# A decoder layer on one core: FFN products that add up in shared PSUM banks, and modulation sums moved ahead

## The chip, the cores and the metric

The kernel runs on one core of a Trainium2 chip. The metric is the device time of one execution in microseconds (us). The engines are TensorE (PE, matmuls; PEld is its weight load), VectorE (DVE), ScalarE (ACT), GpSimd (POOL) and SyncE (SP, whose queue issues the DMAs). PSUM has eight banks of 128 x 512 f32, into which PE writes.

## The reference, cut to what matters

One layer of a decoder: 1024 tokens, width 1024, f32. A conditioning vector `c` gives six modulation rows (`mod = silu(c) @ w_ada + b_ada`): shift, scale and gate for the mixer and for the FFN.

```
mod = c_act @ w_ada[l] + b_ada[l]
sh_m, sc_m, gt_m, sh_f, sc_f, gt_f = ...split(mod, 6)
h = rms_norm(x, g_pre_mix) * (1 + sc_m) + sh_m
x = x + gt_m * rms_norm(mixer(h), g_post_mix)
h = rms_norm(x, g_pre_ffn) * (1 + sc_f) + sh_f
up = h @ w_up                      # 1024 x 5632: gate | val
gate = conv3(gate) + conv_b        # causal, depthwise, along the tokens
y = (gelu_tanh(gate) * val) @ w_down
x = x + gt_f * rms_norm(y, g_post_ffn)
```

The mixer is one input projection, twelve heads of dilated window attention in three groups, a pooling group and an output projection.

## The kernel before, in words

Every f32 matmul operand is split into a high part of type fp32r (`copy`, on ACT) and the low rest (`lower`, `split`, on DVE), and each product is three matmuls: high x high, high x low, low x high (L1044 to L1046 in the FFN's first half, L1344 to L1346 in its second).

**Start** (to 62 us): adaLN columns, first norm, transposes, first projection.

**Attention phase** (to about 385 us): six units, each a pair of heads. `project(un, prev)` runs 8 x 8 groups of three matmuls (L222 to L224); after each group the queue `Q` ticks one slot and runs the tasks that are due: scores (L655), softmax, transposes (L675), weighted sums (L685), merges. PE's program is in the order written; the other engines' order in this phase is set by a scheduler by priority, and earlier code has the higher priority. In units 2, 3 and 4 (`MU = 2`) three modulation rows are computed as well, in halves `hf` of 512 columns: mixer gate (`mod_row`), FFN shift and FFN scale (`mod_col`). `mod_acc` loads eight 128 x 512 blocks into two buffers `mraw` (L485), multiplies and adds them on DVE into one buffer `macc` (L487, L489). PE then sums over partitions with a matmul of ones, 20 slots (first half) and 48 slots (second half) into the unit: L504 for the row, after a split of `macc` into `mah` and `mal`, L519 for columns. The row goes on with two broadcast loads and L508.

**Middle** (385 to 447 us): output projection, norms, transposes of h into the 2 x 2 blocks of the FFN's operand, and the first products.

**FFN, first half** (447 to 860 us): 22 units `c` of 2 x 128 columns (gate and value). Each is a 2 x 2 block product in Winograd's form with seven products instead of eight: `(n, c)`, n = 1 to 7, of 12 matmuls each. Products 1 and 2 run one to three units ahead. `steps` is PE's order: `(5,c) (4,c-1) (6,c) (2,k) (1,k) (3,c) (7,c)`, and for the first and last units `(5,c) (6,c) (4,c-1) (3,c) (7,c)`; the last step is `(4,21)`, right behind `(7,21)`. Each product has a bank of its own, from the list `idle`. `evac(n, c)` adds it on DVE into tiles in SBUF one step later (L1053 to L1063), with `UU` for the sum that several results share; `first(c)` copies product 1 on ACT and adds product 2. After product 4 comes the gate's chain: `cv` on ACT (L1064), two taps on DVE (L1154, L1156), GELU on ACT (L1158), times the value on DVE (L1161, `gated`). `act_sum` (L1173) forms the sums of two units that the second half needs, and SP stores them in `gscr`. All four engines follow the order written here. At the last five steps `prep_down` starts to load and split operands of the second half.

The FFN's gate row is computed in this half too (`gate_acc`, L1197, one block at a step; `gate_sum`, L1204), from unit 14 on.

**FFN, second half** (860 us to the end): again seven products, order `DOWN = (1, 2, 6, 5, 3, 7, 4)`, each over 11 blocks k and 4 blocks of tokens t, in two groups of four banks by turns. `out_sum` adds them up, `y_half` and `y_end` make the last norm, the gate and the residual (L1350 to L1366). In the last product the blocks of tokens end one after another.

Of the kernel before, what the change touches and what calls it, by code (L numbers as in the profile page):

```python
# [79 lines left out]
MU = 2  # L80
# [7 lines left out]
GATE_AT = 16  # L88
# [11 lines left out]
def block_kernel(ctx: ExitStack, tc: tile.TileContext, x, pos, cols, rows, consts, w_ada_a, w_ada_b, w_in_u,  # L100
# [411 lines left out]

    def mod_col(s, mb, hf, use, later):
        acc = mod_acc(s, hf)
        m = bank(mb)

        def fin():
            for i in range(4):
                nc.tensor.matmul(m[:, i:i + 1], acc[:, i * P:(i + 1) * P], ones[:, 0:1], start=True, stop=True)  # L519
            use(m[:, 0:4], slice(4 * hf, 4 * hf + 4))  # L520

        later(fin)
# [51 lines left out]
    with tc.tile_pool(name="bp", bufs=1) as bp, tc.manual_schedule(engines={ET.PE}):  # L574
# [210 lines left out]

        prev = None
        for ui in range(5):
# [11 lines left out]
            if MU <= ui <= MU + 2:  # L799
                for hf in range(2):  # L800
                    due = Q.slot + MLAG[hf]
                    later = lambda f, ahead=False, due=due: Q.at(due - MSPL * ahead, f)
                    if ui > MU:
                        mod_col(ui - MU, 7, hf, fin_shift if ui == MU + 1 else fin_scale, later)
                    elif hf:
                        Q.after(MLAG[0] + 1, lambda later=later: mod_row(0, 2, 6, gtg, 7, 1, later))
                    else:
                        mod_row(0, 2, 6, gtg, 7, 0, later)
# [7 lines left out]
        wps.append(load_piece(w_in_p[0], 1024))  # L816
        attend(un, Q.slot + 24)
# [27 lines left out]
    if True:  # L845
# [88 lines left out]
        with tc.manual_schedule(engines={ET.PE, ET.Activation, ET.DVE, ET.Pool}):  # L934
# [61 lines left out]
            UU = cp.tile([P, 2, 512], F32, name="UU", tag="gtg")  # L996
# [10 lines left out]

            def start_piece(n, src):
                W[n, 0] = new_piece()
                split(src, *W[n, 0])  # L1010
# [25 lines left out]
            def product(n, c):  # L1036
                a, w = USES[n]
                wh, wl = W.pop((w, c))
                used[n, c] = idle.pop(0)
                o = bank(used[n, c])  # L1040
                for k in range(4):
                    ks = slice(k * P, (k + 1) * P)
                    ah, al = side(a, k)
                    nc.tensor.matmul(o, wh[:, ks], ah, start=k == 0, stop=False)  # L1044
                    nc.tensor.matmul(o, wh[:, ks], al, start=False, stop=False)  # L1045
                    nc.tensor.matmul(o, wl[:, ks], ah, start=False, stop=k == 3)  # L1046
# [3 lines left out]
            def evac(n, c):  # L1050
                u, v = UU[:, c % 2], VV[c % 3]
                if n == 6:
                    nc.vector.tensor_sub(u, u, done_with(6, c))  # L1053
                    nc.vector.tensor_add(v[:, hi], u, done_with(5, c))
                elif n == 3:
                    nc.vector.tensor_add(v[:, lo], v[:, hi], done_with(3, c))
                elif n == 7:
                    o = done_with(7, c)
                    nc.vector.tensor_add(u, u, o)
                    nc.vector.tensor_add(v[:, hi], v[:, hi], o)  # L1060
                elif n == 4:
                    g = GG[:, c % 2]
                    nc.vector.tensor_add(g[:, hi], u, done_with(4, c))  # L1063
# [17 lines left out]
            first(1)  # L1081
# [3 lines left out]
            product(3, 0)  # L1085
            sums(hi_t, (3,))
# [8 lines left out]
            evac(6, 0)  # L1095
            start_sum("t4", b21, b21, t2r)
            evac(3, 0)
# [6 lines left out]
    gtf_d = tc.dram_tile([1, D], F32, name="gtf_d")  # L1104
    with tc.manual_schedule(engines={ET.PE, ET.Activation, ET.DVE, ET.Pool}):
# [4 lines left out]
        def fetch(src, low=True):  # L1110
# [3 lines left out]
            if low:  # L1114
                lower(r, *w)
            return w if low else (w, r)

        def lower(r, wh, wl):
            nc.vector.tensor_tensor(wl, r, wh.bitcast(F32), ALU.subtract)  # L1119
# [5 lines left out]
        def prep(n, c):  # L1125
# [10 lines left out]
            elif n in (1, 2):  # L1136
                w, r = fetch(w_up[c, :, n - 1], False)
                W[n, c] = w
                return lambda: lower(r, *w)
# [10 lines left out]
            copy(nc.scalar, w[0], src)  # L1150
            return lambda: lower(src, *w)
# [17 lines left out]
        def act_sum(c, i):  # L1169
            g0, g1 = VV[(c - 1) % 3], VV[c % 3]  # L1170
# [6 lines left out]
        for c in range(NC_FF):  # L1177
# [7 lines left out]
            if c in SKIP or not ahead:  # L1185
                steps += [(5, c), (6, c)] + old + [(3, c), (7, c)]
            else:
                steps += [(5, c)] + old + [(6, c)] + ahead + [(3, c), (7, c)]
        steps.append((4, NC_FF - 1))

        def gate_acc(hf, kb):
            raw, acc = gm[:, 0], gm[:, 1]
            nc.sync.dma_start(raw, w_ada_b[3, hf, kb])
            if kb == 0:
                nc.vector.tensor_scalar_mul(acc, raw, cact2[:, 0:1])
            else:
                nc.vector.scalar_tensor_tensor(acc, raw, cact2[:, kb:kb + 1], acc, op0=ALU.mult, op1=ALU.add)  # L1197
            if kb == 7:
                nc.sync.dma_start(raw[0:1], rows[5:6, hf * 512:(hf + 1) * 512])

        def gate_sum(hf, c):
            used["gate", c] = idle.pop(0)
            o = bank(used["gate", c])
            nc.tensor.matmul(o, ones, gm[:, 1], start=True, stop=True)  # L1204
            row, g, sl = gm[0:1, 0], gm[0:1, 1], slice(hf * 512, (hf + 1) * 512)
            nc.sync.dma_start(g, rows[7:8, sl])

            def add():
                nc.vector.tensor_tensor(row, done_with("gate", c)[0:1], row, ALU.add)

            def fin():
                nc.vector.scalar_tensor_tensor(row, row, -1.0 if hf else 1.0, g, op0=ALU.mult, op1=ALU.mult)
                nc.sync.dma_start(gtf_d[:, sl], row)

            at_step(now[0] + 1, add)
            at_step(now[0] + 3, fin)
# [12 lines left out]
        def finish_4(c):  # L1229
            i, g, v = now[0], GG[:, c % 2], VV[c % 3]  # L1230
# [9 lines left out]
        for hf, c in ((0, GATE_AT), (1, GATE_AT + 3)):  # L1240
            i = steps.index((5, c))
            EXTRA.setdefault(i, []).append(lambda hf=hf, c=c: gate_sum(hf, c))
            for kb in range(8):
                EXTRA.setdefault(i - 14 + kb, []).append(lambda hf=hf, kb=kb: gate_acc(hf, kb))
        for c in range(1, NC_FF - 1):
            EXTRA.setdefault(START_AT[c] + 5, []).append(lambda c=c: at_step(now[0], lambda: first(c + 1)))
# [9 lines left out]
        def prep_down(i):  # L1256
# [20 lines left out]
            split(raw, *w)  # L1277
# [45 lines left out]
    with tc.manual_schedule(engines={ET.PE}):  # L1323
# [3 lines left out]
        gtf = VV[1]  # L1327
        nc.sync.dma_start(gtf, gtf_d.to_broadcast([P, D]))
        O = {}
        for n in ("u", "11", "12", "22"):  # L1330
# [5 lines left out]
        def dbank(n, t):  # L1336
            return bank(idle[4 * (DOWN.index(n) % 2) + t])

        def down(n, t, ks):
            o = dbank(n, t)  # L1340
            ts_ = slice(t * P, (t + 1) * P)
            for k in ks:
                (gh, gl), (wh, wl) = DW[n, k]
                nc.tensor.matmul(o, gh[:, ts_], wh, start=k == 0, stop=False)  # L1344
                nc.tensor.matmul(o, gh[:, ts_], wl, start=False, stop=False)  # L1345
                nc.tensor.matmul(o, gl[:, ts_], wh, start=False, stop=k == KD - 1)  # L1346

        def y_half(T, hf, y):
            sl = slice(hf * 512, (hf + 1) * 512)
            nc.scalar.activation(cv[:, sl], y, AF.Square, accum_out=q2[:, T, hf:hf + 1])  # L1350
            nc.vector.tensor_mul(y, y, gtf[:, sl])

        def y_end(T, ys, order):
# [109 lines left out]
```

## Time and profile before

| | |
|---|---|
| median of 3 runs | 1080.71 us (1079.68 to 1083.68) |
| the profiled execution | 1080.04 us |
| its span, first to last instruction | 1078.3 us |
| PE busy | 1038.9 us, 96% |
| DVE busy | 860.6 us, 80% |
| ACT busy | 474.8 us, 44% |
| POOL busy | 217.9 us, 20% |
| mean granted PE clock | 0.99 |
| DMA | 168.34 MB, mean 156 GB/s |

A row of a group gives line, engine, operation, output and inputs, count, then busy time and mean ns. A row of a timeline gives the start in us from the start of the span, the duration, engine, line and tiles, and in brackets how long the engine was idle before it and what it waited for. A row of waits gives who waited for whom, in us, with the count and the longest. PE's matmuls overlap, so the distance between two starts (0.226 us for 512 columns at full clock) counts, not the duration of one (0.39).

### The profile page before, as it was taken

To read this page: it belongs to the slowest core of one execution; us is meant where nothing else is said; L and a number is where in the kernel's file an instruction comes from. 1 tells how busy PE (TensorE), PEld (TensorE's weight loads), DVE (VectorE), ACT (ScalarE), POOL (GpSimd) and SP (SyncE) were. 2 spreads that over 40 slices of the span, in tenths; PEclk is the share of its full clock that TensorE was granted. 3 is DMA by queue.
4 is the path that set the end of the run, shared out by engine and by line. 5 is a ranking of instruction groups with operands and counts; after the bars stand their busy time and mean duration, and the time that the engine had idled before them with its cause. 6 is when DMAs were issued, how large, how long until landed. Compare 5 with 4: busy or idle time off the path is not lost.

```text
span 1078.3 us, 15477 instructions
## 1 busy us (share of the span) xinstructions
PE 1038.9 (96%) x5174; PEld 876.9 (81%) x5174; DVE 860.6 (80%) x1886; ACT 474.8 (44%) x958; POOL 217.9 (20%) x132
## 2 busy tenths in 40 slices
PE   4899999999999999999999999999999999999996
PEld 4898988898888877777888888888878888888885
DVE  8975466885457779999999888979789999756997
ACT  6564332433354469534433333432223455544541
POOL 0000000000000000063433333323235525003360
PEclk9999999999999999999999999999999999999999
DMA  9652346353131163323344424344434889566653
GB/s 361 212 154 74 114 112 193 94 174 91 53 94 51 30 235 137 118 88 131 120 160 140 164 100 155 118 150 163 166 117 138 287 290 383 161 196 207 225 173 117
DMA packets 85148, 168.34 MB, mean 156 GB/s; under 512 B 9158, under 2 KB 25926, under 8 KB 81356
## 3 DMA queue, kind: packets, MB, share of 16 engines
q1 hardware_dynamic: 85068, 167.35, 46.7%
q8 instruction: 41, 0.67, 0.3%
q14 instruction: 39, 0.32, 0.1%
HBM read 134.47 MB, written 32.84 MB: 155 GB/s over the span
## 4 chain that ended last, share of the span: by engine, by line
PE 73%; DVE 16%; DMA 5%; ACT 3%; issue 2%; SPq 0%; POOL 0%; DVEq 0%; ACTq 0%; POOLq 0%
PE PS L1044 9%; PE PS L1045 9%; PE PS L1046 9%; PE PS L1345 6%; PE PS L1344 6%; PE PS L1346 6%; PE PS L222 5%; PE PS L224 5%; PE PS L223 5%; PE PS L685 3%; PE PS L655 2%; DMA gm<-in_w_ada_b_dram 2%; DMA mraw<-in_w_ada_b_dram 2%; PE PS L675 1%; DVE more L1119 1%
## 5 line engine op out<-in xcount | busy, mean ns | idle before, releaser
L1123 POOL TENSOR_TENSOR raws<-rw 128x512 f32<-128x512 f32 x30 | 45.5, 1516 | 512.5 <-DVE t2r L1068 450.3
L222 PE MATMUL PS<-wh,hh 128*128 128x384 f32 x336 | 125.4, 373 | 0.0
L224 PE MATMUL PS<-wh,hl 128*128 128x384 f32 x336 | 113.9, 339 | 0.0
L223 PE MATMUL PS<-wl,hh 128*128 128x384 f32 x336 | 113.7, 338 | 0.0
L118 ACT ACTIVATE more<-raws 128x512 fp32r<-128x512 f32 x81 | 49.6, 624 | 67.0 <-PE PS L1045 53.1
L1119 DVE TENSOR_TENSOR more<-raws,more 128x512 fp32r<-128x512 f32 x75 | 71.7, 958 | 3.1 <-ACT more L118 3.1
L664 ACT ACTIVATE pm<-pm,nm 128x128 f32<-128x128 f32 (+1 forms) x96 | 42.4, 443 | 65.0 <-DVE nm L662 43.8
L222 PEld LDWEIGHTS PS<-wh,hh 128*128 128x128 f32 x336 | 64.0, 190 | 7.9 <-issue 4.8
L223 PEld LDWEIGHTS PS<-wl,hh 128*128 128x128 f32 x336 | 64.0, 191 | 0.6 <-issue 0.5
L224 PEld LDWEIGHTS PS<-wh,hl 128*128 128x128 f32 x336 | 63.7, 189 | 0.0
L1064 ACT ACTIVATE cv<-GG,col 128x1024 f32<-128x1024 f32 x22 | 27.4, 1245 | 76.0 <-DVE GG L1063 76.0
L1044 PE MATMUL PS<-a,more 128*128 128x512 f32 x144 | 56.1, 390 | 1.3 <-DVE VV L1060 1.3
L1046 PE MATMUL PS<-a,more 128*128 128x512 f32 x144 | 56.3, 391 | 1.0 <-DVE more L1119 1.0
L1045 PE MATMUL PS<-a,more 128*128 128x512 f32 x144 | 56.0, 389 | 0.0
L658 DVE CUSTOM_DVE_ANT_0 pm<-PS,cst 128x128 f32<-128x128 f32 (+1 forms) x96 | 30.8, 348 | 29.7 <-PE PS L655 22.6
L1345 PE MATMUL PS<-tail 128*128 128x512 f32 x128 | 49.9, 390 | 0.0
L1344 PE MATMUL PS<-tail 128*128 128x512 f32 x128 | 49.8, 389 | 0.0
L1346 PE MATMUL PS<-tail 128*128 128x512 f32 x128 | 49.8, 389 | 0.0
L1158 ACT ACTIVATE cv<-cv 128x1024 f32<-128x1024 f32 x22 | 23.4, 1062 | 57.9 <-DVE cv L1156 57.9
L1154 DVE SCALAR_TENSOR_TENSOR cv<-GG,col,cv 128x1023 f32<-128x1023 f32 x22 | 36.9, 1678 | 11.4 <-ACT cv L1064 11.4
L170 DVE TENSOR_TENSOR wl<-raw,wh 128x768 fp32r<-128x768 f32 (+1 forms) x34 | 34.8, 1033 | 12.0 <-ACT wh L118 11.8
L489 DVE SCALAR_TENSOR_TENSOR macc<-mraw,cact,macc 128x512 f32<-128x512 f32 x42 | 31.4, 748 | 15.6 <-DMA mraw<-in_w_ada_b_dram 15.4
(389 smaller groups left out, 3102.5 us busy)
## 6 DMA issues: line engine op xcount, KB each, us to landing
rw<-in_w_up_dram SPq DMA_DIRECT2D x21, 1024.0 KB
gscr<-VV SPq DMA_DIRECT2D x66, 256.0 KB
mraw<-in_w_ada_b_dram SPq DMA_DIRECT2D x48, 256.0 KB
R<-in_w_down_dram SPq DMA_DIRECT2D x48, 256.0 KB
raw<-in_w_in_u_dram SPq DMA_DIRECT2D x24, 384.0 KB
wa<-in_w_ada_a_dram SPq DMA_DIRECT2D x8, 1024.0 KB
R<-gscr SPq DMA_DIRECT2D x27, 256.0 KB
raws<-in_w_up_dram SPq DMA_DIRECT2D x25, 256.0 KB
```

The source lines that it names most:

```text
L118: nc.scalar.activation(o, i, AF.Copy)
L222: nc.tensor.matmul(o, a, wh[:, c0:c0 + 384], start=k == 0, stop=False)
L223: nc.tensor.matmul(o, a, wl[:, c0:c0 + 384], start=False, stop=False)
L224: nc.tensor.matmul(o, b, wh[:, c0:c0 + 384], start=False, stop=k == 7)
L1044: nc.tensor.matmul(o, wh[:, ks], ah, start=k == 0, stop=False)
L1045: nc.tensor.matmul(o, wh[:, ks], al, start=False, stop=False)
L1046: nc.tensor.matmul(o, wl[:, ks], ah, start=False, stop=k == 3)
L1119: nc.vector.tensor_tensor(wl, r, wh.bitcast(F32), ALU.subtract)
L1123: nc.gpsimd.tensor_tensor(t, a, b, ALU.add)
L1344: nc.tensor.matmul(o, gh[:, ts_], wh, start=k == 0, stop=False)
L1345: nc.tensor.matmul(o, gh[:, ts_], wl, start=False, stop=False)
L1346: nc.tensor.matmul(o, gl[:, ts_], wh, start=False, stop=k == KD - 1)
```

## The change

1. *Shared banks in the first half.* Product 6 adds into the bank that still holds product 1 (with its weights negated), then 7 and 4 add into the same bank; product 3 adds into the bank of 5. The partial sums are read out in between: ACT copies after 5, 6 and 4, DVE adds after 3 and 7. `UU` is gone. The order of a full unit is now `(5,c) (6,c) (4,c-1) (2,k) (1,k) (3,c) (7,c)`.
2. *Shared banks in the second half.* The same for `DOWN`: 6 and 7 on the banks of 1, 3 on those of 5. Part of the work of `out_sum` moves to `out_more`, after all four blocks, and the loads for later steps are issued after `out_sum` at the end of a product.
3. *Buffers.* A third gate tile (in `gm`, where the FFN's gate row was summed) and a fourth value tile (in the place of `UU`).
4. *Modulation sums.* Mixer gate in unit 1, FFN shift in unit 2, FFN scale in unit 4 (`MODS`). The FFN's gate row is computed by the new `mod_gate` after the pool product that precedes unit 5's projection.
5. *Last norm.* The same number of small DVE operations per block, one of them now ahead of the one that needs the square root.

```diff
-MU = 2
+MODS = {1: 0, 2: 1, 4: 2}
...
-GATE_AT = 16
...
+    def mod_gate(hf, mb, later):
+        acc = mod_acc(3, hf)
+        sl = slice(hf * 512, (hf + 1) * 512)
+        parts = []
+
+        def parted():
+            for name in ("mah", "mal"):
+                parts.append(mr[0].tile([P, 512], F32R, name=name, tag="mraw", bufs=2))
+            split(acc, *parts)
+
+        def fin():
+            for i in range(2):
+                nc.tensor.matmul(bank(mb), onesr, parts.pop(0), start=i == 0, stop=i == 1)
+            row, g = (mr[0].tile([P, 512], F32, name="mraw", tag="mraw", bufs=2)[0:1] for _ in range(2))
+            nc.sync.dma_start(row, rows[5:6, sl])
+            nc.sync.dma_start(g, rows[7:8, sl])
+            nc.vector.tensor_tensor(row, bank(mb)[0:1], row, ALU.add)
+            nc.vector.scalar_tensor_tensor(row, row, -1.0 if hf else 1.0, g, op0=ALU.mult, op1=ALU.mult)
+            nc.sync.dma_start(gtf_d[:, sl], row)
+
+        later(parted, True)
+        later(fin)
...
+        def mods_of(m):
+            for hf in range(2):
+                due = Q.slot + MLAG[hf]
+                later = lambda f, ahead=False, due=due: Q.at(due - MSPL * ahead, f)
+                if m in (1, 2):
+                    mod_col(m, 7, hf, (fin_shift, fin_scale)[m - 1], later)
+                    continue
+                go = (lambda hf=hf, later=later: mod_gate(hf, 7, later) if m else mod_row(0, 2, 6, gtg, 7, hf, later))
+                if hf:
+                    Q.after(MLAG[0] + 1, go)
+                else:
+                    go()
...
-            if MU <= ui <= MU + 2:
...
+            if ui in MODS:
+                mods_of(MODS[ui])
...
         pool(1, wps[0], r2.tile([P, PAD + S], F32, name="u1", tag="r2b"), 14)
         wps.append(load_piece(w_in_p[0], 1024))
+        mods_of(3)
         attend(un, Q.slot + 24)
...
-            UU = cp.tile([P, 2, 512], F32, name="UU", tag="gtg")
+            VV.append(cp.tile([P, S], F32, name="VV3", tag="gtg"))
...
+            def gate_of(c):
+                return GG[:, c % 3] if c % 3 < 2 else gm[:, 0:2].rearrange("p a b -> p (a b)")
...
             def first(c):
...
-                copy(nc.scalar, UU[:, c % 2], done_with(1, c))
-                nc.vector.tensor_add(GG[:, c % 2, 0:512], UU[:, c % 2], done_with(2, c))
+                g = gate_of(c)[:, 0:512]
+                copy(nc.scalar, g, bank(used[1, c]))
+                nc.vector.tensor_add(g, g, done_with(2, c))
...
             def product(n, c):
...
-                used[n, c] = idle.pop(0)
-                o = bank(used[n, c])
+                on = {3: 5, 4: 1, 6: 1, 7: 1}.get(n)
+                if not on:
+                    used[n, c] = idle.pop(0)
+                o = bank(used[on or n, c])
...
-                    nc.tensor.matmul(o, wh[:, ks], ah, start=k == 0, stop=False)
+                    nc.tensor.matmul(o, wh[:, ks], ah, start=not on and k == 0, stop=False, skip_group_check=True)
...
             def evac(n, c):
-                u, v = UU[:, c % 2], VV[c % 3]
-                if n == 6:
-                    nc.vector.tensor_sub(u, u, done_with(6, c))
-                    nc.vector.tensor_add(v[:, hi], u, done_with(5, c))
+                v = VV[c % 4]
+                if n == 5:
+                    copy(nc.scalar, v[:, hi], bank(used[5, c]))
+                elif n == 6:
+                    copy(nc.scalar, v[:, lo], bank(used[1, c]))
                 elif n == 3:
-                    nc.vector.tensor_add(v[:, lo], v[:, hi], done_with(3, c))
+                    nc.vector.tensor_add(v[:, lo], v[:, lo], done_with(5, c))
                 elif n == 7:
-                    o = done_with(7, c)
-                    nc.vector.tensor_add(u, u, o)
-                    nc.vector.tensor_add(v[:, hi], v[:, hi], o)
+                    nc.vector.tensor_add(v[:, hi], v[:, hi], bank(used[1, c]))
                 elif n == 4:
-                    g = GG[:, c % 2]
-                    nc.vector.tensor_add(g[:, hi], u, done_with(4, c))
+                    g = gate_of(c)
+                    copy(nc.scalar, g[:, hi], done_with(1, c))
                     nc.scalar.activation(cv, g, AF.Identity, bias=cl("conv_b", c), scale=cl("conv_w2", c))
...
             product(6, 0)
-            first(1)
+            evac(5, 0)
...
             product(3, 0)
+            evac(6, 0)
...
-            if c in SKIP or not ahead:
-                steps += [(5, c), (6, c)] + old + [(3, c), (7, c)]
-            else:
-                steps += [(5, c)] + old + [(6, c)] + ahead + [(3, c), (7, c)]
+            steps += [(5, c), (6, c)] + old + ([] if c in SKIP else ahead) + [(3, c), (7, c)]
         steps.append((4, NC_FF - 1))
-
-        def gate_acc(hf, kb):
...
-        def gate_sum(hf, c):
...
         def later_evac(n, c):
-            if n in (3, 4, 6, 7):
+            if n > 2:
                 at_step(now[0] + LAG_EV, lambda: (evac(n, c), finish_4(c) if n == 4 else None))
...
         def dbank(n, t):
-            return bank(idle[4 * (DOWN.index(n) % 2) + t])
+            return bank(idle[4 * (n in (2, 3, 4, 5)) + t])
...
-            r0, v = newton(sd, lambda v: nc.vector.tensor_scalar(v, q[:, a:a + 1], 1.0 / D, q[:, 2:3], op0=ALU.mult,
-                                                                 op1=ALU.add))
-            nc.vector.tensor_scalar_mul(q[:, 3:4], v, r0)
+            r0 = sp.tile([P, 1], F32, name="r0", tag="sm_r0")
+            v = sp.tile([P, 1], F32, name="v", tag="sm_v")
+            nc.vector.tensor_scalar(v, q[:, a:a + 1], 1.0 / D, q[:, 2:3], op0=ALU.mult, op1=ALU.add)
+            nc.vector.reciprocal(r0, sd)
+            nc.vector.tensor_scalar(v, v, r0, r0, op0=ALU.mult, op1=ALU.mult)
+            nc.vector.tensor_scalar_mul(r0, r0, -0.5)
+            nc.vector.scalar_tensor_tensor(q[:, 3:4], v, -3.0, r0, op0=ALU.add, op1=ALU.mult)
```

More of the change, by code (lines that the diff above doesn't have):

```diff
@@ L1149, in prep @@
             w = W[key, c] = new_piece()
-            copy(nc.scalar, w[0], src)
-            return lambda: lower(src, *w)
+            high(key, w[0], src)
+            return lambda: lower(key, w, src)
         def taps(c, g):
@@ L1399, in block_kernel @@
             ks = range(k, KD) if n == DOWN[-1] and k == KD - ENDS else (k,)
-            for t in range(4):
-                down(n, t, ks)
-                if ks[-1] == KD - 1:
-                    out_sum(n, t)
+            for stage in range(2):
+                if stage == last:
+                    while ready < i + AHEAD_D:
+                        prep_down(ready)
+                        ready += 1
+                if stage:
+                    break
+                for t in range(4):
+                    down(n, t, ks)
+                    if ks[-1] == KD - 1:
+                        out_sum(n, t)
+            if last:
+                for t in range(4):
+                    out_more(n, t)
 def _host(inputs):
```

127 lines of the change are left out of this document (53 added, 74 removed).

## The prediction

> **What bounds the kernel.** I read the page first, then the groups of waits of TensorE (PE), then windows around the few places where it waits, then the order of VectorE (DVE), ScalarE (ACT) and the DMA queue (SP) at the places that the change touches.
>
> ```profile
> span 1078.3 us, 15477 instructions
> PE 1038.9 (96%) x5174; PEld 876.9 (81%) x5174; DVE 860.6 (80%) x1886; ACT 474.8 (44%) x958; POOL 217.9 (20%) x132
> ```
>
> PE is busy for 96% of the span. A gain can come only from the 39 us in which it is idle, from stages at a lower clock, or from matmuls that go away. The execution took 1080.04 us, 1.7 more than its span and 0.7 under the median of the runs, 1080.71. I sum against 1080.04.
>
> ```profile
> PE PS L1045 <- DVE s3l L170: 2.1, 1, 2.1
> PE PS L1046 <- DVE more L1119: 1.4, 3, 0.5
> PE PS L1044 <- DVE VV L1060: 1.3, 1, 1.3
> PE PS L655 <- DVE U L658: 1.2, 1, 1.2
> PE PS L519 <- DVE macc L489: 1.2, 2, 0.8
> PE PS L1046 <- DVE p L1119: 0.6, 1, 0.6
> 182.00:192.00 10.00, 9.07 (x37) 7.80 (x38) 6.88 (x43) 2.66 (x11) 0.00 (x0) 0.66 0.42 116
> 462.00:468.00 6.00, 5.34 (x16) 4.24 (x17) 4.40 (x7) 0.84 (x2) 2.17 (x2) 0.72 0.26 87
> ```
>
> In a wait row stand the total, the number of times and the longest; in a window the busy time of PE, PEld, DVE, ACT, POOL, then PE's granted clock. A wait costs twice: after the 1.2 and 0.8 us waits at 181 to 184 us the clock is 0.66 over 10 us, which loses 0.34 x 10 = 3.4 us more; after the 2.1 us wait at 461 us it is 0.72 over 6 us, which loses 1.7. The Trainium skill (TensorE: Matmul & The Clock Gate, What's actually happening) has the clock halve after at least one idle window of about 3.4 us; here waits of 2.1 us in sum were enough, so I go by the windows. By the page's rule a wait below 3.4 us would cost no clock, and the sum below would be 1.7 lower, at its row wait.
>
> **The change, part by part.**
>
> *Gate row out of the FFN.* Sixteen loads, 16 DVE sums and two PE sums leave the FFN.
>
> ```profile
> DVE gm L1197 <- DMA gm<-in_w_ada_b_dram: 18.5, 12, 4.9
> L1204 PE MATMUL PS<-gm,onesr 128*128 128x512 f32 x4 | 2.0, 590 | 0.0
> L504 PE MATMUL PS<-mah,onesr 128*128 128x512 f32 x2 | 0.9, 449 | 0.0
> L504 PE MATMUL PS<-mal,onesr 128*128 128x512 f32 x2 | 0.8, 396 | 0.0
> 260.00:310.00 50.00, 50.00 (x294) 43.28 (x294) 25.28 (x90) 22.32 (x61) 0.00 (x0) 1.00 0.24 69
> ```
>
> DVE stood 18.5 us before gate loads, with the low halves (L1119) queued behind it, and PE waited for those 1.4 + 0.6 = 2.0 us. They go: -2.0. The four matmuls of L1204 (2.0 us) are replaced by four like those of L504 (0.9 + 0.8): -0.3. In the attention phase the new sums run after the scale sums, in unit 5 with the pool product before it, where (260 to 310 us) PE has no wait, DVE is busy for 25.3 of 50 us and the DMA for 0.24; the matmuls come 20 and 48 slots on. I cost them at nothing; if the scores queue behind a load on DVE, as at L655 above, 1.2.
>
> *Shared banks.* Products 6, 7 and 4 add into the bank of 1, and 3 into that of 5. Four DVE operations a unit fall away and three ACT copies come.
>
> ```profile
> 600.00:700.00 100.00, 100.00 (x443) 82.84 (x442) 87.73 (x104) 37.33 (x53) 33.21 (x21) 1.00 0.39 132
> L1060 DVE TENSOR_TENSOR VV<-VV,PS x22: 673/675/681, 469.5 to 870.0; 128x512 f32<-128x512 f32 x22
> L118 ACT ACTIVATE UU<-PS x22: 575/578/582, 445.6 to 842.7; 128x512 f32<-128x512 f32 x22
> ```
>
> In a unit of 19 us that is 4 x 0.675 = 2.7 us off DVE and 3 x 0.578 = 1.7 onto ACT. PE is busy 100.00 of 100 us there, so in the middle of the FFN this relief buys nothing. What is added is a wait: a product that adds to a bank must wait until the partial sum in it has been read. In the middle there are two products, 5.4 us, between 7 of a unit and its 4, and DVE then has the add done in 2 us. The banks no longer run short, so the wait for L1060 goes: -1.3. Early on, where DVE is behind, I checked unit 1:
>
> ```profile
> 480.50 0.39 PE L1044 MATMUL PS<-s,p 128*128 128x512 f32 x1
> 483.06 2.20 DVE L1156 SCALAR_TENSOR_TENSOR cv<-GG,col,cv 128x1022 f32<-128x1022 f32 x1
> ```
>
> Its 7 has ended at 480.5, its 4 would start at 485.9. After the taps (end 485.3) DVE does the sum of 3, one low half and the sum of 7, 2.0 us, to 487.3; but seven evictions of 0.6 have left its queue by then (4.2 us), so 483.1 and no wait; with half of the relief, none either. At the start of the FFN one DVE eviction of 0.6 leaves the queue ahead of s3l, on which PE waits 2.1: -0.6 (between -1.2 and +1.5, since ACT now copies product 6 before s3).
>
> *The last product.* Unit 21 is the last, and nothing lies between its 7 and its 4: (4,21) adds to the bank that DVE has still to read. In program order, DVE does before that read: the taps of unit 20, the sum of 3, two low halves for the down stage, the gating of unit 20.
>
> ```profile
> 851.59 0.39 PE L1046 MATMUL PS<-b,p 128*128 128x512 f32 x1
> 857.03 0.39 PE L1046 MATMUL PS<-s3h,more 128*128 128x512 f32 x1
> 857.25 0.39 PE L1044 MATMUL PS<-b,more 128*128 128x512 f32 x1
> 855.36 0.63 ACT L118 ACTIVATE p<-R 128x512 fp32r<-128x512 f32 x1 [0.73 <-DMA R<-in_w_down_dram]
> 860.27 1.25 ACT L1064 ACTIVATE cv<-GG,col 128x1024 f32<-128x1024 f32 x1 [4.29 <-DVE GG L1063]
> 861.55 1.52 DVE L1154 SCALAR_TENSOR_TENSOR cv<-GG,col,cv 128x1023 f32<-128x1023 f32 x1 [1.38 <-ACT cv L1064]
> 863.10 2.20 DVE L1156 SCALAR_TENSOR_TENSOR cv<-GG,col,cv 128x1022 f32<-128x1022 f32 x1
> 865.40 1.06 ACT L1158 ACTIVATE cv<-cv 128x1024 f32<-128x1024 f32 x1 [3.88 <-DVE cv L1156]
> 867.62 0.68 DVE L170 TENSOR_TENSOR more<-gm,more 128x512 fp32r<-128x512 f32 x1
> 868.22 1.22 DVE L1161 SCALAR_TENSOR_TENSOR VV<-cv,VV 128x1024 f32<-128x1024 f32 x1
> 869.96 0.68 DVE L1060 TENSOR_TENSOR VV<-VV,PS 128x512 f32<-128x512 f32 x1
> ```
>
> Before, DVE ended the read at 870.6 while PE went on at 857.3 in another bank. After, the chain is the same but starts sooner. Upper end: the ACT copy comes behind the ACT copy of 855.36, so cv (L1064) starts at 856.6 instead of 860.3, 3.7 sooner, and one add is gone (0.6): 866.3, plus 0.1 to PE, a wait of 9.1. Lower end: nothing on ACT is in the way and the chain starts where (4,20) ends, 852.0: 0.1 + 0.6 copy + 1.2 cv + 3.7 taps + 1.1 GELU + 0.6 copy + 1.3 low halves + 1.2 gating + 0.6 add = 862.4, a wait of 5.2. ACT's copies there wait for loads that were issued behind DVE's late act sums, and DVE will be less late: I take the middle, +7.0. PE then runs slow as at 462 us: +1.7 (up to 3.4 if two such stretches follow, as at 182 us). The Trainium skill (PSUM — Partial Sum Buffer, PSUM bank collisions) says that the hardware does not arbitrate between PE and a reader in one bank, so the wait is not to be had cheaper; no run here shows that.
>
> *Sums a unit sooner.* The row sums go to unit 1, shift to unit 2, scale stays in unit 4. PE meets the first row matmul 20 slots into unit 1, at 84.7 us.
>
> ```profile
> 84.71 0.34 PE L224 MATMUL PS<-wh,hl 128*128 128x384 f32 x1
> 66.30 0.34 SPq L485 DMA_DIRECT2D mraw<-in_w_ada_b_dram  x1
> 85.88 0.42 SPq L485 DMA_DIRECT2D mraw<-in_w_ada_b_dram  x1
> 70.00:74.00 4.00, 4.00 (x27) 3.94 (x27) 2.83 (x12) 1.14 (x3) 0.00 (x0) 1.00 0.87 267
> 88.57 0.75 DVE L489 SCALAR_TENSOR_TENSOR macc<-mraw,cact,macc 128x512 f32<-128x512 f32 x1 [0.63 <-DMA mraw<-in_w_ada_b_dram]
> 90.02 0.69 DVE L170 TENSOR_TENSOR mal<-macc,mah 128x512 fp32r<-128x512 f32 x1
> ```
>
> The first half of the row was already summed as early as its loads allowed, from 66.3 to 90.7 us, 40 us before its use. With use at 84.7, and nothing changed in that order, PE waits 6.1 us. The loads now stand ahead of unit 1's own stores in the queue, so they may come sooner, but they and the next unit's weights run at 0.87 of the DMA: 2.0 at the least if the last load goes out 4 us sooner, none at all if more. I take 2.0, since the order of priority changed, and 1.7 for the clock: +3.7. From the second row matmul to the shift sums the chain is that of before, moved from units 2 and 3 to 1 and 2; its waits of 1.2 and 0.8 and their 3.4 of clock stay: 0. The scale sums have a unit of their own before them: -0.4, the rest of L519's 1.2.
>
> *Third gate, fourth value buffer.* They hold data longer; no wait row names such a buffer: 0.
>
> *The end.* PE ends at 1069.67, DVE at 1075.4:
>
> ```profile
> 1061.28 0.74 DVE L1366 SCALAR_TENSOR_TENSOR o<-o,q,rw 128x512 f32<-128x512 f32 x1
> 1069.28 0.39 PE L1346 MATMUL PS<-tail 128*128 128x512 f32 x1
> 1074.65 0.75 DVE L1366 SCALAR_TENSOR_TENSOR o<-o,q,rw 128x512 f32<-128x512 f32 x1
> ```
>
> The second L1366 of a block returns after (1074.65 - 1061.28) / 3 = 4.46 us, against 18 matmuls x 0.226 = 4.06 on PE, so DVE sets the pitch. One small operation moves off the chain behind the square root in each of four blocks, 0.1 to 0.2 us: -0.5 (0 to -1.0). In the down stage product 3 adds to 5's bank after an ACT copy of 0.6, with 9 matmuls (2.0 us) between: 0.
>
> Sum: -2.0 - 0.3 - 1.3 - 0.6 + 8.7 + 3.7 - 0.4 - 0.5 = +7.3, so 1087.3 us.
>
> **Rivals.**
> *Not slower, inside 0.5%:* the row loads come more than 6 us sooner and PE finds its row ready. Without the 3.7 the sum is 1083.6. It decides where the last row load issues: before about 80 us.
> *Faster:* with the attention sums early every wait there goes (1.2 + 0.8 + 3.4), DVE's relief removes the s3l wait (2.1 + 1.7, less the 0.6 counted), and the last product is at its lower end (5.2): 1083.6 - 5.4 - 3.2 - 1.8 = 1073.2. For it: DVE is the late engine at 461 us. Against it: the relief comes mostly after that place.
> *Much slower:* row and last product at their upper ends with two slow stretches each: 1087.3 + 4.1 + 1.7 + 2.1 + 1.7 = 1096.9.
>
> **How the numbers follow.** A measurement here tells about 0.5% (5.4 us) from no change. Waits at both places, 1084 to 1092: 0.43; much slower: 0.09; together slower 0.52. No row wait, or both small: 0.32. Faster: 0.16. The range leaves out 2 in 10: from 1074 to 1097; that of the likeliest alone is 1084 to 1092.
>
> **What would show it.** Right: a PE wait of 5 to 9 us for a DVE read of VV, once, near the end of the products, with a clock of 0.5 behind it; a PE wait for mah or mal near 85 us; no DVE wait for gate loads in the FFN; DVE's busy time down by about 60 us and the FFN no shorter for it in its middle. Wrong: if PE passes its last product within 2 us, or the row matmuls without a wait, I have misread an order on DVE or SP; if ACT's added copies hold up products 3, 6 or 7 in the middle, the loss is larger than I say.

## The result, and the profile after

The changed kernel takes 1092.32 us (median of 6 runs, 1091.56 to 1094.51); the kernel before takes 1080.75 beside it (6 runs, 1079.04 to 1084.91). The ratio is 1.0105, with a 95% interval of 1.009 to 1.0121: 11.6 us slower. The profiled execution took 1093.12 us, 13.1 more than the one of before. The page of the changed kernel begins:

```profile
span 1091.3 us, 15426 instructions
PE 1041.0 (95%) x5174; PEld 879.8 (81%) x5174; DVE 801.9 (73%) x1788; ACT 517.4 (47%) x1038; POOL 211.4 (19%) x132
```

DVE is busy for 59 us less and ACT for 43 more, and PE executes as many matmuls as before. The waits of PE in the changed kernel (total, times, longest), those that the change made or left:

```profile
PE PS L1093 <- DVE VV L1108: 6.6, 2, 6.3
PE PS L679 <- DVE U L682: 3.3, 1, 3.3
PE PS L503 <- ACT mah L117: 2.9, 1, 2.9
PE PS L699 <- ACT kT L117: 2.3, 2, 1.8
PE PS L1094 <- DVE s3l L169: 2.1, 1, 2.1
PE PS L1093 <- ACT s3h L117: 1.7, 1, 1.7
```

L1093 is the first matmul of a product and L1094 the second, L1108 the read of product 7, L503 the row's matmul, L699 a transpose, L679 a score and L682 its mask. Windows of the changed kernel (busy time of PE, PEld, DVE, ACT, POOL, then granted clock and DMA share): unit 1, unit 2, unit 3 of the attention phase, the stretches behind three waits, and the middle and the end of the FFN's first half.

```profile
73.80:128.80 55.00, 50.04 (x294) 45.20 (x293) 31.47 (x110) 19.82 (x61) 0.00 (x0) 0.94 0.53 145
128.80:188.00 59.20, 54.94 (x330) 49.73 (x329) 34.10 (x114) 18.56 (x57) 0.00 (x0) 0.94 0.49 143
188.00:241.50 53.50, 52.99 (x339) 47.38 (x339) 41.32 (x235) 22.16 (x72) 0.00 (x0) 1.00 0.24 69
88.00:95.00 7.00, 6.30 (x20) 5.16 (x20) 2.54 (x12) 2.01 (x8) 0.00 (x0) 0.51 0.28 75
146.00:153.00 7.00, 7.00 (x28) 6.24 (x28) 2.85 (x12) 1.94 (x8) 0.00 (x0) 0.51 0.41 128
870.00:877.00 7.00, 4.24 (x11) 3.38 (x12) 3.91 (x4) 0.00 (x0) 1.81 (x2) 0.53 0.52 170
600.00:700.00 100.00, 100.00 (x443) 82.81 (x442) 70.51 (x81) 44.08 (x68) 33.90 (x22) 1.00 0.38 127
794.00:848.00 54.00, 54.00 (x240) 44.70 (x239) 37.99 (x42) 24.98 (x38) 16.01 (x9) 1.00 0.44 148
```

Units 1 and 2 now have waits and half clock, as unit 3 had before (the same view of the kernel before, its unit 3):

```profile
169.50:230.30 60.80, 58.16 (x356) 52.14 (x355) 49.67 (x254) 21.91 (x72) 0.00 (x0) 0.94 0.44 127
```

The middle of the FFN is as long as before with 17 us less of DVE in 100 us. The place of each difference follows from the starts of the same matmuls in both traces. The columns are lengths of a stage in us, "end" being from product 140 (its third matmul) to the last matmul; the other kernels are those of the experiments, in their order below.

| | before | changed | e1 | e2 | e3 | e4 | e5 | e6 | e7 | e8 | f1 | f2 |
|---|---|---|---|---|---|---|---|---|---|---|---|---|
| unit 1 | 45.8 | 55.0 | 45.6 | 54.5 | 46.1 | 52.9 | 54.3 | 51.5 | 53.0 | 45.6 | 45.6 | 56.2 |
| unit 2 | 50.3 | 59.2 | 50.2 | 57.6 | 50.0 | 58.4 | 56.0 | 62.3 | 50.9 | 50.3 | 50.0 | 54.9 |
| unit 3 | 60.7 | 53.5 | 57.1 | 53.5 | 57.4 | 53.5 | 56.0 | 53.5 | 53.5 | 57.1 | 56.5 | 53.5 |
| unit 4 | 60.5 | 59.9 | 61.3 | 59.7 | 62.4 | 59.9 | 62.7 | 59.9 | 59.6 | 61.9 | 60.8 | 59.7 |
| unit 5 | 58.2 | 59.1 | 59.1 | 59.1 | 59.3 | 58.2 | 59.1 | 59.1 | 59.1 | 59.1 | 59.1 | 59.1 |
| products 100 to 139 | 113.9 | 108.8 | 108.8 | 108.8 | 108.8 | 114.1 | 108.8 | 108.8 | 108.8 | 108.8 | 108.8 | 108.8 |
| end | 225.2 | 233.4 | 234.5 | 225.1 | 225.1 | 227.7 | 234.4 | 233.9 | 234.2 | 225.1 | 225.1 | 231.2 |

So the five units cost 11.1 us more (10.2 in units 1 to 4, 0.9 in unit 5), products 100 to 139 (where the gate row was) 5.1 less, the end 8.3 more. What is left is small: +0.3 before unit 1 and +0.5 in the middle, where nothing was changed, -0.7 and -1.2 at the start of the FFN, 0.0 from product 20 to 99, -0.2 behind the last matmul. They add up to the 13.0 us between the spans.

The timeline of PE in the changed kernel, where the row's matmul comes:

```profile
85.09 0.49 PE L679 MATMUL PS<-kT,qT 64*128 64x128 f32 x4
88.45 0.80 PE L503 MATMUL PS<-mah,onesr 128*128 128x512 f32 x1 [2.87 <-ACT mah L117]
```

And the timeline of DVE in the same kernel, 55 us later:

```profile
143.44 0.75 DVE L488 SCALAR_TENSOR_TENSOR macc<-mraw,cact,macc 128x512 f32<-128x512 f32 x1 [3.74 <-DMA mraw<-in_w_ada_b_dram]
144.12 0.28 DVE L682 CUSTOM_DVE_ANT_0 pm<-PS,cst 128x128 f32<-128x128 f32 x1
```

At 85.6 us PE stands before the row's matmul. At 141.2 it stands before a score (the 3.3 us for L682): DVE's order has a sum of the shift ahead of that mask, and DVE stands 3.74 us until the raw block has landed. At the last product, the timeline of DVE in the changed kernel:

```profile
859.26 1.77 DVE L1048 TENSOR_TENSOR more<-R,more 128x512 fp32r<-128x512 f32 x1
860.95 1.78 DVE L1048 TENSOR_TENSOR p<-R,p 128x512 fp32r<-128x512 f32 x1
862.66 2.31 DVE L1199 SCALAR_TENSOR_TENSOR cv<-gm,col,cv 128x1023 f32<-128x1023 f32 x1
865.00 1.28 DVE L1201 SCALAR_TENSOR_TENSOR cv<-gm,col,cv 128x1022 f32<-128x1022 f32 x1
866.20 0.68 DVE L1106 TENSOR_TENSOR VV<-VV,PS 128x512 f32<-128x512 f32 x1
867.99 1.32 DVE L1048 TENSOR_TENSOR more<-R,more 128x512 fp32r<-128x512 f32 x1 [1.10 <-ACT more L117]
869.23 0.68 DVE L1048 TENSOR_TENSOR more<-gm,more 128x512 fp32r<-128x512 f32 x1
869.84 2.28 DVE L1206 SCALAR_TENSOR_TENSOR VV<-cv,VV 128x1024 f32<-128x1024 f32 x1
872.03 0.68 DVE L1108 TENSOR_TENSOR VV<-VV,PS 128x512 f32<-128x512 f32 x1
```

Beside it, the timelines of GpSimd and of ACT (one row, the first step of the gate's chain):

```profile
858.74 1.74 POOL L1283 TENSOR_TENSOR R<-R,gm 128x512 f32<-128x512 f32 x1
860.44 3.45 POOL L1283 TENSOR_TENSOR R<-R,raws 128x512 f32<-128x512 f32 x2
867.50 1.27 POOL L1283 TENSOR_TENSOR R<-R,rw 128x512 f32<-128x512 f32 x1 [3.61 <-DMA R<-in_w_down_dram]
869.30 1.73 POOL L1283 TENSOR_TENSOR R<-R,rw 128x512 f32<-128x512 f32 x1 [0.54 <-DMA R<-in_w_down_dram]
857.92 1.25 ACT L1112 ACTIVATE cv<-gm,col 128x1024 f32<-128x1024 f32 x1
```

Product (7,21) ended at 862.2 and its read at 872.7, so the read was 10.5 us late. PE filled 4.2 us of that with 18 matmuls of the down stage, which its order now had ahead of (4,21), and waited 6.3. In the code (4,21) is still written ahead of the down stage; what moved those matmuls is not shown.

### The profile page after: what moved, and what is told of

The parts are those of the page before. It is cut to its first block, busy times and chain, and to the rows that moved or that the text cites. A ratio compares the mean times of both kernels' runs of the same rounds, so it can differ in the third digit from the quotient of the medians.

```text
span 1091.3 us, 15426 instructions
## 1 busy us (share of the span) xinstructions
PE 1041.0 (95%) x5174; PEld 879.8 (81%) x5174; DVE 801.9 (73%) x1788; ACT 517.4 (47%) x1038; POOL 211.4 (19%) x132
## 4 chain that ended last, share of the span: by engine, by line
PE 76%; DVE 13%; DMA 6%; ACT 3%; issue 2%; SPq 0%; DVEq 0%; ACTq 0%
PE PS L1095 12%; PE PS L1093 12%; PE PS L1094 12%; PE PS L1356 6%; PE PS L1355 6%; PE PS L1357 6%; PE PS L221 5%; PE PS L223 4%; PE PS L222 4%; PE PS L709 2%; DMA mraw<-in_w_ada_b_dram 2%; PE PS L679 2%; PE PS L699 1%; DVE acc L338 1%; DVE x L900 1%
## 5 line engine op out<-in xcount | busy, mean ns | idle before, releaser
L1168 POOL TENSOR_TENSOR raws<-rw 128x512 f32<-128x512 f32 x30 | 46.1, 1538 | 572.6 <-PE PS L1095 462.0
L688 ACT ACTIVATE pm<-pm,nm 128x128 f32<-128x128 f32 (+1 forms) x96 | 42.4, 443 | 68.8 <-DVE nm L686 52.0
L117 ACT ACTIVATE more<-raws 128x512 fp32r<-128x512 f32 x70 | 43.5, 626 | 61.7 <-PE PS L1094 53.2
L1048 DVE TENSOR_TENSOR more<-raws,more 128x512 fp32r<-128x512 f32 x70 | 61.0, 878 | 14.8 <-ACT more L117 14.8
L682 DVE CUSTOM_DVE_ANT_0 pm<-PS,cst 128x128 f32<-128x128 f32 (+1 forms) x96 | 30.8, 348 | 38.1 <-PE PS L679 30.0
L488 DVE SCALAR_TENSOR_TENSOR macc<-mraw,cact,macc 128x512 f32<-128x512 f32 x56 | 41.9, 748 | 19.9 <-DMA mraw<-in_w_ada_b_dram 19.7
L1093 PE MATMUL PS<-a,more 128*128 128x512 f32 x144 | 56.0, 389 | 0.0
L1094 PE MATMUL PS<-a,more 128*128 128x512 f32 x144 | 56.0, 389 | 0.0
L265 ACT ACTIVATE qs<-PS 128x256 f32<-128x256 f32 x48 | 18.2, 382 | 51.8 <-PE PS L223 47.0
L117 ACT ACTIVATE wh<-raw 128x768 fp32r<-128x768 f32 (+1 forms) x34 | 30.7, 905 | 20.6 <-DMA raw<-in_w_in_u_dram 14.8
```

What stands on the lines that cost most here:

```text
L117: nc.scalar.activation(o, i, AF.Copy)
L1048: nc.vector.tensor_tensor(w[1], src, w[0].bitcast(F32), ALU.subtract)
L1093: nc.tensor.matmul(o, wh[:, ks], ah, start=not on and k == 0, stop=False, skip_group_check=True)
L1094: nc.tensor.matmul(o, wh[:, ks], al, start=False, stop=False, skip_group_check=True)
L1168: nc.gpsimd.tensor_tensor(t, a, b, ALU.add)
```

## The experiments

The theory after the comparison: two losses, apart in time, each with one cause. The sums a unit sooner make DVE stand before raw loads with PE's operands behind them; the last product waits for a read that is late in DVE's order. The rivals: the gate row in the attention phase is what costs there; DVE is late at the end whatever the bank; and for the gain, the shared banks' relief of DVE and not the gate row. Medians are beside those of the kernel before that ran on the same chip (1082.02, 1080.24 and 1080.22 us in the three groups: e1 to e4, e5 to e8, f1 and f2).

**e1: the units back.**
```diff
-MODS = {1: 0, 2: 1, 4: 2}
+MODS = {2: 0, 3: 1, 4: 2}
```


> The changed kernel with the row, shift and scale sums back in units 2, 3 and 4; the gate row stays in unit 5. Theory (the unit sooner costs what the attention phase lost): units 1 to 4 took 10.2 us more in the changed kernel (+9.2, +8.9, -7.3, -0.7), and that goes: 1092.3 - 10.2 = 1082.1. The waits of TensorE for mah (2.9) and for the scores' L682 (3.3) disappear, and the old 1.2 and 0.8 before the shift sums return. Rival (the gate row that joined the attention phase is what costs): it stays within 2 us of 1092.3.

Measured: 1080.74 us, ratio 0.9989 (0.9971 to 1.0006). Units 1 and 2 are those of the kernel before, and unit 5 still has the 0.9 us of the gate row. The theory holds, and the gate row is cleared: four matmuls' worth and no wait.

Unit 3, though, takes 57.1 us and not 60.7, with the same sums in it. Ahead of the shift's first sum PE waits for 1.4 us in all, where it waited for 2.1 in the kernel before, and the clock holds behind it:

```profile
182.00:192.00 10.00, 8.58 (x54) 7.04 (x54) 8.94 (x52) 3.88 (x16) 0.00 (x0) 1.00 0.51 149
```

The same view of the kernel before, in the prediction, has 0.66. In e3 and e8, where the sums are in unit 3 as well, the waits are 1.7 and 1.2 us, the clock is 1.00 too, and the unit takes 57.4 and 57.1. So about 3.4 us of unit 3's 60.7 is a stretch of half clock that these three executions do not have; whether their shorter waits or chance spared them is not shown. The 10.2 us are then too low a price: against e1, e3 and e8 the sums a unit sooner cost 11.7 to 13.4 us in units 1 to 4, and the ratios of e1 and the changed kernel lie 1.16% apart, 12.5 us.

**e2: a bank of its own for the last product.** VectorE adds it to a copy of bank 1 that ScalarE makes after product 7.
```diff
-on = {3: 5, 4: 1, 6: 1, 7: 1}.get(n)
+on = {3: 5, 4: 1 if c < NC_FF - 1 else None, 6: 1, 7: 1}.get(n)
...
+# evac(7, 21), behind the sum:
+copy(nc.scalar, gate_of(c)[:, hi], done_with(1, c))
...
+# evac(4, 21):
+nc.vector.tensor_add(g[:, hi], g[:, hi], done_with(4, c))
```


> The changed kernel, but the last product (4,21) has a bank of its own again, as in the kernel before, and VectorE adds it to a copy of the shared bank. Theory (the wait for the shared bank is the loss of the end): the 6.3 us wait at 866 us and the half clock behind it go, and the end costs what it did before: 8.3 us less, 1084.0. Rival (VectorE is late there whatever the bank, and the lateness comes out as another wait of TensorE in the down stage): 1088 to 1092, with a new wait for VectorE's low halves after 870 us.

Measured: 1084.42 us, ratio 1.0017 (0.9998 to 1.0036). The end takes 225.1 us, as before. DVE in this kernel, at the same place:

```profile
865.87 0.68 DVE L1106 TENSOR_TENSOR VV<-VV,PS 128x512 f32<-128x512 f32 x1
867.66 1.78 DVE L1048 TENSOR_TENSOR more<-R,more 128x512 fp32r<-128x512 f32 x1 [1.11 <-ACT more L117]
869.96 2.31 DVE L1206 SCALAR_TENSOR_TENSOR VV<-cv,VV 128x1024 f32<-128x1024 f32 x1
872.20 0.68 DVE L1108 TENSOR_TENSOR VV<-VV,PS 128x512 f32<-128x512 f32 x1
874.00 0.67 DVE L1111 TENSOR_TENSOR GG<-GG,PS 128x512 f32<-128x512 f32 x1
```

DVE reads as late as in the changed kernel, and PE does not wait: the lateness of DVE costs nothing where no product needs the bank. The rival falls.

**e3: both.**


> Both of the other two edits in one kernel: sums back in units 2, 3 and 4, and a bank of its own for the last product. Theory (the two losses are apart in time and add): 1092.3 - 10.2 - 8.3 = 1073.8, which is 0.6% under the kernel before; what is left is the gain of the FFN, about -7. Rival (the two losses overlap, or the FFN's gain needs the earlier sums): not under 1079.

Measured: 1073.27 us, ratio 0.9914 (0.9893 to 0.9935), 0.5 us from the forecast, or 2.3 by the ratio, since the kernel before was slower in this group. The losses add, and the rest of the change is a gain of 0.9%.

**e4: the units alone, on the kernel before.**
```diff
-if MU <= ui <= MU + 2:        # row 2, shift 3, scale 4
+if ui in {1: 0, 2: 1, 4: 2}:  # row 1, shift 2, scale 4 (unit: sums)
```


> The kernel before with one part of the change alone: row sums in unit 1, shift sums in unit 2, scale sums in unit 4; the gate row stays in the FFN and no bank is shared. Theory: the loss of units 1 to 4 comes with this part alone, 1080.75 + 10.2 = 1091.0. Rival (it takes the gate row or the rest of the change to bring it): under 1084.

Measured: 1093.45 us, ratio 1.0107 (1.0076 to 1.0138). This part alone slows the kernel before. By the trace, units 1 to 5 account for 7.3 us of it; the end of this execution was 2.5 longer too. Among PE's waits is one that the kernel before does not have, for low halves in the down stage:

```profile
PE PS L1345 <- DVE tail L170: 1.5, 3, 0.8
```

The starts of the matmuls around these three waits lie 2.4 us further apart than without them, which is nearly all of the 2.5. Why DVE is late there is not shown.

**e5: only the row a unit sooner.**
```diff
-MODS = {1: 0, 2: 1, 4: 2}
+MODS = {1: 0, 3: 1, 4: 2}
```


> The changed kernel with only the row sums a unit sooner (unit 1); the shift sums go back to unit 3, unit 2 has none. Theory (each set of sums costs in the unit that it is moved into): unit 1 stays at 55.0 us, unit 2 falls to that of the kernel before less the row's four matmuls, 50.3 - 1.7 = 48.6, unit 3 is again 60.7; the sum of the three is 164.3 against 167.6 in the changed kernel, so 1089.0. Rival (the row's lateness runs on into unit 2, and the shift costs nothing there): unit 2 stays near 57, and the time is over 1096.

Measured: 1093.23 us, ratio 1.012 (1.0091 to 1.0149): neither. Unit 2 took 56.0 us, although no shift sum is due there. The timeline of its DVE shows why:

```profile
144.33 0.75 DVE L488 SCALAR_TENSOR_TENSOR macc<-mraw,cact,macc 128x512 f32<-128x512 f32 x1 [4.41 <-DMA mraw<-in_w_ada_b_dram]
145.93 0.42 DVE L682 CUSTOM_DVE_ANT_0 pm<-PS,cst 128x256 f32<-128x256 f32 x1
```

The shift's loads and sums start as soon as `macc` is free of the row, whatever unit they are written in; only PE's matmul stays in its unit. So a set of sums does not cost in "its" unit: the row's place sets when the shift's sums stand in DVE's order.

**e6: the row's matmuls later.**
```diff
-due = Q.slot + MLAG[hf]
+due = Q.slot + (MLAG[hf] if m else (28, 56)[hf])
...
-Q.after(MLAG[0] + 1, go)
+Q.after((MLAG[0] if m else 28) + 1, go)
```


> The changed kernel with the matmuls of the row sums due later in unit 1: 28 and 56 slots into it and not 20 and 48; the loads of the first half stay where they are. Theory (TensorE came to the row 2.9 us too early): that wait and the stretch of half clock behind it go, 6.5 us: 1085.8. Rival (VectorE and the loads are the bound of unit 1, and the later use only moves the wait to the scores): not under 1090, with new waits for scores or transposes before 120 us.

Measured: 1092.78 us, ratio 1.0114 (1.0083 to 1.0145). My number was wrong. The wait for the row is gone, and the next set pays for it, as PE's waits show:

```profile
PE PS L543 <- DVE macc L488: 5.5, 1, 5.5
PE PS L679 <- DVE U L682: 2.2, 2, 1.5
```

The later row holds `macc` longer and the shift's sums start 1.5 us later (127.92 us and 126.41), but the last of them comes when it did, at 144.19 and 144.32. The timeline of DVE in e6:

```profile
144.19 0.75 DVE L488 SCALAR_TENSOR_TENSOR macc<-mraw,cact,macc 128x512 f32<-128x512 f32 x1 [1.32 <-DMA mraw<-in_w_ada_b_dram]
```

PE came to unit 2 3.9 us sooner and waits 5.5 us for that sum (unit 2: 62.3 us). The chain of loads and sums is the bound of units 1 and 2, as the rival had it, though most of the wait came back at the shift: new before 120 us are only 0.7 for a score and 1.0 for transposes.

**e7: eight buffers for the raw loads.** They take memory that is unused from unit 1 to unit 4.
```diff
-raw = mr[0].tile([P, 512], F32, name="mraw", tag="mraw", bufs=2)
+raw = big[kb // 4][:, kb % 4]   # two tiles of 128 x 4 x 512
```


> The changed kernel with eight buffers for the raw loads of the row, shift and scale sums, where it has two: all eight loads of a half can go out at once. Theory (each load waits for VectorE to free one of two buffers, and VectorE then stands 1 to 4 us before it, with the scores behind): the last load goes out before 75 us and not at 84, the waits at 85 us and 141 us go with their half clocks: 2.9 + 3.3 + 6.8 = 13.0 less some 3 that stay: about 1082. Rival (the DMA is the bound; its share is 0.86 to 0.92 from 72 to 84 us and from 132 to 144, and the weights of the next unit go out ahead): the loads land no sooner, and the time stays within 2 us of 1092.3.

Measured: 1084.63 us, ratio 1.0041 (1.0024 to 1.0059): 7 us less than the changed kernel by the ratios. The first row matmul runs without a wait and unit 2 takes 50.9 us. One wait of 3.84 is new in unit 1, in the timeline of PE (L509 is the row here, L685 a score, L688 its mask):

```profile
87.05 0.50 PE L509 MATMUL PS<-mah,onesr 128*128 128x512 f32 x1
97.35 0.70 PE L685 MATMUL PS<-kT,qT 64*128 64x128 f32 x4 [3.84 <-DVE U L688]
```

The timeline of DVE has the row's bias (L513) ahead of that mask:

```profile
94.06 0.69 DVE L513 TENSOR_TENSOR gtg<-PS,mraw 128x512 f32<-128x512 f32 x1 [2.96 <-DMA mraw<-in_rows_dram]
```

That of the queue has the raw loads (L490) ahead of the bias (L512), and the window from 84 to 90 us shows the DMA at 0.95:

```profile
83.28 2.47 SPq L490 DMA_DIRECT2D big<-in_w_ada_b_dram  x5
87.85 0.90 SPq L512 DMA_DIRECT2D mraw<-in_rows_dram  x2
```
```profile
84.00:90.00 6.00, 6.00 (x36) 5.17 (x36) 5.91 (x23) 3.24 (x9) 0.00 (x0) 1.00 0.95 312
```

The raw loads, now free to go out, fill the DMA ahead of the row's two bias loads. So two buffers were most of the loss: the DMA is not the bound that the rival made of it, but it is the next one.

**e8: the gate row alone, on the kernel before.** `gate_acc` and `gate_sum` leave the FFN, `mod_gate` is added in unit 5; no bank is shared.


> The kernel before with one part of the change alone: the gate row's sums in unit 5 of the attention phase and not in the FFN; no bank is shared and the other sums stay where they were. Theory (the gain of products 100 to 140, 5.1 us, is that of the gate row alone; it costs 0.9 in unit 5): 1080.75 - 5.1 + 0.9 = 1076.5, and the wait of 1.3 us for VV at 489 us stays. Rival (the relief by shared banks brings that gain): 1080 to 1082.

Measured: 1075.2 us, ratio 0.9952 (0.9932 to 0.9972). Products 100 to 139 take 108.8 us as in the changed kernel, and among PE's waits the one of L1060 for the sum of product 7 is as it was (L1077 and L1093 here):

```profile
PE PS L1077 <- DVE VV L1093: 1.3, 1, 1.3
```

The gain is the gate row's. Shared banks take DVE from 80% to 73% of the span and bring 1.3 to 1.9 us, in products 0 to 19: these take 64.8 us in the kernel before and in e8, and 62.9 to 63.5 in the kernels with shared banks.

**f1: e3 with eight buffers.**


> Sums back in units 2, 3 and 4, a bank of its own for the last product, and eight buffers for the raw loads. Theory (VectorE standing before raw loads is also what unit 3 and unit 4 of the kernel before pay for): units 3 and 4 took 57.4 and 62.4 us with these sums and two buffers, 53.5 and 59.7 where no sums stood in the way; 4 to 6 us go from 1073.3: about 1068. Rival (in units 2 to 4 TensorE's waits are only 2.2 us in all, the rest of those units is work): not under 1071.

Measured: 1070.56 us, ratio 0.9907 (0.9887 to 0.9928). This is between the two: units 3 and 4 got 2.6 us shorter against e3, not 4 to 6, and the intervals of e3 and f1 overlap. Both are faster than the two kernels that were compared.

**f2: the shared bank, read first.**
```diff
-later_evac(n, c)
+evac(n, c) if (n, c) == (7, NC_FF - 1) else later_evac(n, c)
```


> The changed kernel with the shared bank kept, but VectorE's read of (7,21) stands in its order straight after the sum of 3, ahead of two low halves and the gating of unit 20. Theory (the wait is what is queued ahead of the read on VectorE, not the bank as such): the read ends near 867.5 and not at 872.7, the wait of 6.3 us falls to 1, and the clock holds: 1092.3 - 5.2 - 3.4 = 1083.7. Rival (VectorE is late at that place because of the work before it, the low halves beside GpSimd, and the order of the last four operations matters little): not under 1089.

Measured: 1089.41 us, ratio 1.009 (1.006 to 1.0121). The forecast was missed, and the time is the one that the rival gave. The timeline of DVE:

```profile
863.28 0.68 DVE L1106 TENSOR_TENSOR VV<-VV,PS 128x512 f32<-128x512 f32 x1
863.88 0.68 DVE L1108 TENSOR_TENSOR VV<-VV,PS 128x512 f32<-128x512 f32 x1
```

And the wait of PE:

```profile
PE PS L1093 <- DVE VV L1108: 4.2, 1, 4.2
```

The read does end 5.2 us sooner (864.56; products run 2.9 ahead of the changed kernel's in this trace, so 867.5 on its scale). But in PE's order only 4 of the 18 down matmuls now stand ahead of (4,21): 1.1 us of cover and not 4.2. So the wait fell by 2.1, and the end by 2.2; the clock did not hold (0.72 from 864 to 870 us). What is queued ahead of the read on DVE is the cause, as the theory had it; I had not asked what else the order would move.

## Why the prediction was right or wrong

The direction was right, and the cause of the slowdown named at both places; the sum was 7.3 us and the measured difference 11.6 (13.1 between the profiled executions), because one term was put at a third of its size or less. The time lies inside the range, 0.3 us above the 1084 to 1092 of the likeliest case. Against the profiled executions: 7.3, +6.9 for the sums a unit sooner, -1.9 for the gate row, -0.4 for the last product, +0.3 for the end, +0.8 where nothing was changed, 13.0.

*Gate row:* predicted -2.3 net. By the traces -5.1 in the FFN and +0.9 in unit 5. The FFN loses the whole of its four matmuls (two sums of 0.87 us: products 100 to 119 took 55.27 us in the kernel before, with one of them, and 54.40 without), not the 0.3 of a replacement, whose other side lies in unit 5. And I took waits for costs: a wait counts from a matmul's modelled end, 0.39 us after its start, where the next would have started after 0.226, so each of four waits cost 0.16 more than it showed. And the matmul behind the one that waited starts 0.34 us later and not 0.226 (789.00 and 789.34 us for the first), another 0.45 in all. Some 0.2 of the 5.1 remains without a name. No score waited behind the gate's loads.

*Shared banks:* predicted -1.3 for L1060's wait, measured -1.2 (products 8 to 19). At the FFN's start -0.6 was predicted and -0.7 measured, for another reason. The wait for s3l stayed at 2.1, and the hazard that I named, ACT's copy of product 6 ahead of s3, came (1.7 us for s3h); the gain is one stretch of half clock less, and that is no fixed gain: in e1, e2, e5, e7 and f2 the half clock behind the same waits lasts 6.8 us and not 3.4, and products 0 to 7 take 0.2 to 0.5 us more than in the kernel before. ACT's copies never held up products in the middle: PE is busy for 100.00 of 100 us.

*The last product:* predicted +8.7, measured +8.3; e2 takes away all of it. That it came so near is luck: the parts were off both ways. The read was 10.5 us late, past my upper end of 9.1. ACT was not in the way: `cv` ended at 859.2, 0.3 us behind my lower end. But DVE stood in two low halves that I had in no term (859.26 and 860.95, 1.77 and 1.78 us), so the taps began at 862.66; and behind the taps one low half took 1.32 us and not 0.68, and the gating 2.28 and not 1.22. All four stand beside sums of GpSimd. And 18 down matmuls covered 4.2 us, which I had not seen: I took the order of PE there to be as it was.

*Sums a unit sooner:* predicted +3.3 (row +3.7, shift 0, scale -0.4), measured +11.1 over units 1 to 5, 0.9 of it the gate row, and more against e1, e3 and e8. This is the step that failed. The row's wait was 2.9 + 0.2 where I took 2.0, inside the bounds. The clock behind it was half for 6.8 us, so some 3 us and not 1.7. A transpose 28 us later waited another 1.8 for kT. The words that broke are "moved from units 2 and 3 to 1 and 2; its waits of 1.2 and 0.8 and their 3.4 of clock stay: 0". I moved a chain and kept its waits. Unit 3 did get 7.3 us shorter (3.4 of it the clock, as e1 shows), but unit 2 got 8.9 longer: DVE stood 3.74 us before a raw load with the scores behind it. e5 and e6 show that the chain from the row to the shift is one, through `macc`, and e7 that two buffers set its pace.

*The end:* predicted -0.5, measured -0.2 behind the last matmul.

## What to carry to other kernels

When an accumulator and its two load buffers feed several sums in turn, moving the first sum moves all of them, and a consumer's due time moves the wait but not the chain; count the chain's loads against what stands behind each on the summing engine. A shared bank cost nothing here while two products (5.4 us) lay between a partial sum and the next product into it, and had to be given up for the last product, where only part of the read's lateness was covered. Before crediting a bundle of edits, run its parts alone: here one part, the gate row, held most of the gain and two small places all of the loss.

## What the runs showed of the hardware that I had not expected

The clock's answer to a wait of some 2 us varies. The same wait of 2.1 us at 55.5 us stands in e1 and in e8. The window behind it in e1:

```profile
55.00:61.00 6.00, 3.94 (x18) 3.62 (x17) 2.41 (x6) 5.24 (x8) 0.00 (x0) 0.72 0.26 71
```

And in e8:

```profile
55.00:61.00 6.00, 3.91 (x26) 3.59 (x25) 2.74 (x6) 5.21 (x8) 0.00 (x0) 1.00 0.25 80
```

In e1 the clock is half for 3.4 us behind it, in e8 it holds. In the changed kernel, e3, e2 and f1 the FFN begins with the same waits of 1.75 and 2.10; the half clock behind them lasts 3.4 us in the changed kernel, e3 and f1, and 6.8 in e2. Every stretch of half clock within the kernels' work is a multiple of 3.41 us. The Trainium skill (TensorE: Matmul & The Clock Gate, What's actually happening) has free-running windows of 3413 ns, and the multiples agree; that an idle window of that length is needed does not, since waits of 2.1 were enough here. So one execution can differ from another by 1.7 us at each such wait (by 3.4 in unit 3 of the kernel before, beside e1), and a wait near 2 us is priced by a chance and not by a constant.

GpSimd beside DVE: the same subtraction of 128 x 512 took 0.68 us alone (867.62 in the kernel before, in the prediction) and 1.77 or 1.78 beside a sum on GpSimd (859.26 and 860.95 above). That is not so in every case: the one at 867.99 took 1.32, beside a GpSimd record that ends at 868.77, and the one at 869.23 took 0.68, although a GpSimd record starts at 869.30. The Trainium skill (Trainium Architecture — The Big Picture, What this means for kernel authors) states an exclusive lock of the port that these two share, which fits the long ones.
